# Two-layer hybrid trunk on one core: the carried part of a chunk's output enters its PSUM bank by four transposes ahead of the chunk-internal products, and its last piece is scaled earlier

## The chip, the cores and the metric

The kernel runs on 1 core of one Trainium2 chip. The metric is device time in microseconds (us) of one execution; a comparison takes the medians of several executions of both kernels on the same chip. All arithmetic is fp32, part of it as fp32r halves (see below).

## The reference, cut to what matters

One inference step of two layers over 384 rows (256 of a prompt, 8 x 16 of samples). The layer is: a modulated norm, one wide input projection, three mixers side by side (windowed attention, a Mamba-2 scan, a gated MLP over chunks), a gated merge, an output projection, then a squared-ReLU MLP. The change lies in the Mamba-2 scan:

```python
def ssd_scan(x, dt, a, bm, cm, h0):
    ...
    cb = jnp.einsum('bctgn,bcsgn->bctsg', cc, bc)
    y_intra = jnp.einsum('bctsg,bctsgk,bcsgkp->bctgkp', cb, decay, xdt)
    ...
    y_inter = jnp.einsum('bctgn,bcgkpn->bctgkp', cc, h_in) * jnp.exp(cum)[..., None]
    y = (y_intra + y_inter).reshape(bsz, s, SSM_HEADS, SSM_HEAD_DIM)
    return y, h_last.reshape(bsz, SSM_HEADS, SSM_HEAD_DIM, SSM_STATE)
```

`y_intra` is the chunk-internal part, `y_inter` the part that the carried state gives.

## The kernel before, in words

The 384 rows are three pieces of 128 columns: i = 0 and 1 are the prompt, i = 2 the eight samples. Activations lie with channels on partitions, so every projection is a row of *units*: a unit is one weight block of 128 x 1024 (`raw`, fetched by SP), split by `split` (from L142) into a high half `whi` (ACT, L147) and a low half `wlo` (DVE, L148), and used in 24 matmuls of 384 columns (in PSUM banks `acc`, three of them). Such matmuls fill TensorE nearly all the time. `mm` at L92 records almost every matmul, so the rows are told apart by their tiles.

The scan is the generator `ssd(g)`, run once for each of two head groups (g = 0, 1) in each layer. `side()` advances it by one step ahead of each unit of the branch projections (`gate`, `half_branch`) and of the z projection (the loop that ends in L1047), so that its small matmuls stand between units. In one `ssd(g)`:

- `scaled(i)` turns four x blocks by transposes (L135) and makes `xdt` (DVE, L835) and from it `xde` (POOL, L836). `bts` is the turned B; the matmuls `mx<-tm,bts` ("bts(0)", "bts(1)") take `xde[0]` and `xde[1]` to the states.
- The carried part of piece 1 is one matmul with `s0`, scaled by DVE into `yin[1]` (L858). That of piece 2 is `carried`, for n = 0 and 1, into the bank `yi`; DVE scales it into `yin[2]` (L954), before the change after the loop over the eight samples.
- `decay` builds two operands for a mask, one on POOL and one on DVE (both L878); `mask` multiplies them with `s1r` on TensorE, takes the exponential (ACT, L887) and multiplies by `cbm` (DVE, L888).
- `sample(b)` updates one sample's state: `bm` from `stack` (DVE, L919), one matmul, POOL (L922), DVE (L923), and the output by SP (L924). `stack` tiles are written by DMAs from `btr` and `xr` (L868, L869); the states `st` come by DMA (L928).
- `within(i)` makes the output of piece i in the one bank `yy`: eight products of 64 x 128 (`xdt` times mask), and for i = 1 and 2 the carried part, by four matmuls of `yin[i]` with the identity (`yy<-cn,tm`; `cn` holds the identity). DVE adds it to x (L907).

With i = 1 and 2, two groups and two layers there are eight such places, with 32 identity matmuls. After the z loop `rs = sq.rstd` makes the norm of the scan's output: matmuls `mx<-ones,sqa`, a square root on ACT (L321, L327, each with loads of function tables), matmuls `mx<-ck,ones`; then come the gates' `tanh` (L1007).

The order of all instructions on each engine's queue is set at build time by a scheduler that works through a model of the program; each queue then runs in that order. Tiles come from pools: `tm` has 11 buffers, the PSUM tags `mx` 3, `yy` 1 and `yi` 1, `stack`, `bm` and `st` two each. When a buffer is held longer, the scheduler gives later tiles other buffers, with other waits.

Of the kernel before, what the change touches and what calls it, by code (L numbers as in the profile page):

```python
# [13 lines left out]
ALU = mybir.AluOpType  # L14
# [48 lines left out]
def trunk_kernel(ctx, tc, x_in, c_in, w_ada, sm_in, gf_in, cn_in, wst, wkv, gmc, kc_in, vc_in, hs_in, cs_in,  # L63
                 y_out, kp_out, vp_out, sp_out, ks_out, vs_out, ss_out, co_out, gv_out):
    nc = tc.nc
    pe, act, dve, pool, sp = nc.tensor, nc.scalar, nc.vector, nc.gpsimd, nc.sync
# [5 lines left out]
    def nm(s):  # L72
        ids[0] += 1
        return f"{s}{ids[0]}"
# [10 lines left out]
    def yi():  # L85
        return psum("yi", 1)

    def yy():
        return psum("yy", 1)

    def mm(out, lhsT, rhs, start, stop):
        return pe.matmul(out, lhsT, rhs, start=start, stop=stop, skip_group_check=True)  # L92

    def behind(ins, other, wait=False):

        kind = mybir.DependencyClass.Sync if wait else mybir.DependencyClass.NoSync
        tc.add_manual_dep(ins.ins, other.ins.name, mybir.DependencyInfo(kind, mybir.DependencyReason.DATA), reason="behind")
# [25 lines left out]
    def const(name):  # L123
        o, w = CN[name]
        return cn[:, o:o + w]

    ident, t1, t1s, s1, s1s, sel, selq = (const(n) for n in ("ident", "t1", "t1s", "s1", "s1s", "sel", "selq"))
    cos, sin = (const(n).rearrange("p (i d) -> p i d", i=3) for n in ("cos", "sin"))

    def small(l, name):  # L130
        o, w = SM[name]
        return sm[:, l, o:o + w]
# [71 lines left out]
    def bc(ap, shape, axis):  # L204
        return ap.unsqueeze(axis).to_broadcast(list(shape))
# [270 lines left out]
    def mixers(l, pa, st, h, first):  # L476
        def tm(dt=F32):
            return pa.tile([128, 512], dt, tag="tm", name=nm("tm"), bufs=11)
# [121 lines left out]
        ecum = [ex[:, i * 16:i * 16 + 16] for i in range(3)]  # L600
# [170 lines left out]
        o = SM["conv_w"][0]  # L771
# [30 lines left out]
        def heads(ap):  # L802
            return ap.rearrange("p (h d) -> p h d", h=8)

        def hb_(ap):
            return bc(ap, (128, 8, 64), 2)

        def ssd(g):
            Bf, Cf = xs[8 + g], xs[10 + g]
            hs = slice(8 * g, 8 * g + 8)  # L810
# [8 lines left out]
            for q in range(2):  # L819
                o = cpad[:, q].rearrange("p (r q t) -> p r q t", r=4, q=2)[:, :, q]  # L820
# [7 lines left out]
            xdt, xde = [], []  # L828
# [26 lines left out]
            yin = {1: tm()}  # L855
# [7 lines left out]
            def stack(j):  # L863

                d, r = pa.tile([128, 640], F32R, tag="stack", name=nm("stack"), bufs=2), slice(32 * j, 32 * j + 32)
                df = d.bitcast(F32)
                for o, xs_, bs_ in ((0, 0, 0), (32, 1, 0), (64, 0, 1)):
                    sp.dma_start(out=df[o:o + 32, 0:512], in_=xr[xs_][r].bitcast(F32))  # L868
                    sp.dma_start(out=df[o:o + 32, 512:], in_=btr[r, bs_].bitcast(F32))  # L869
                act.copy(d[:96, 0:512], df[:96, 0:512])  # L870
                return d


            def decay(hq, i):
                h0 = 8 * g + 4 * hq
                rs = [tm(F32R).rearrange("p (h t) -> p h t", h=4) for _ in range(2)]
                for j, e in enumerate((pool, dve)):
                    e.tensor_tensor(  # L878
                        rs[j], bc(t1, (128, 4, 128), 1), bc(dtr[:, j, i, h0:h0 + 4].bitcast(F32), (128, 4, 128), 2), ALU.mult)
                return rs  # L880

            def mask(hq, i, rs):
                p = mx()
                for j in range(2):
                    mm(p, s1r, rs[j].rearrange("p h t -> p (h t)"), j == 0, j == 1)
                m = tm().rearrange("p (h t) -> p h t", h=4)
                act.activation(m, p.rearrange("p (h t) -> p h t", h=4), AF.Exp)  # L887
                return m, dve.tensor_tensor(m, m, bc(cbm[:, i], (128, 4, 128), 1), ALU.mult)  # L888

            def within(i, masks):  # L890
                p = yy()
                yb = [p[:, c * 128:(c + 1) * 128] for c in range(4)]
                ms = []
                for c in range(4):
                    for hh in range(2):
                        o = (2 * c + hh) * 64
                        ms.append(mm(yb[c][64 * hh:64 * hh + 64], xdt[i][:, o:o + 64], masks[c // 2][0][:, 2 * (c % 2) + hh], c == 0, i == 0))
                behind(ms[0], masks[1][1], True)
                for m in ms[1:]:
                    behind(m, ms[0])  # L900
                if i:
                    for c in range(4):
                        mm(yb[c], yin[i][:, c * 128:(c + 1) * 128], ident, False, True)
                for c in range(4):
                    k = 4 * g + c
                    y = xs[k][:, cols[i]]
                    dve.scalar_tensor_tensor(y, y, small(l, "dskip")[:, k:k + 1], yb[c], ALU.mult, ALU.add)  # L907


            py = yi()  # L910

            def carried(q, st):
                for j in range(4):
                    r = slice(32 * j, 32 * j + 32)
                    mm(py[r, :], cpad[:, q, r], st[:, j], q == 0, q == 1)

            def sample(b, hb, d):
                bm = pa.tile([128, 128], F32R, tag="bm", name=nm("bm"), bufs=2)
                dve.tensor_scalar(bm[:96], d[:96, 512:].bitcast(F32), selq[:96, b % 2:b % 2 + 1], None, ALU.mult)  # L919
                p = mx()  # L920
                mm(p, bm[:96], d[:96, 0:512], True, True)
                pool.tensor_tensor(heads(hb), heads(hb), hb_(decb[:, b, hs]), ALU.mult)  # L922
                dve.tensor_tensor(hb, hb, p, ALU.add)  # L923
                sp.dma_start(out=ss_out[l, :, b, half], in_=hb)  # L924
# [8 lines left out]
            masks = []  # L933
            for n in range(8):
                if n < 2:
                    carried(n, sts[n])
                if n < 4:
                    masks.append(mask(n % 2, n // 2, rs))
                    if n < 3:
                        rs = decay((n + 1) % 2, (n + 1) // 2)  # L940
                if n:
                    b = n - 1
                    sample(b, sts[b % 2][:, b // 2], ds[0])
                    if b % 2:
                        ds.pop(0)
                        if b // 2 < 2:
                            ds.append(stack(b // 2 + 2))
                if n in (2, 4):
                    within(n // 2 - 1, masks[:2])
                    masks = masks[2:]  # L950
                yield
            sample(7, sts[1][:, 3], ds[0])
            yin[2] = tm()
            dve.tensor_tensor(heads(yin[2]), heads(py), hb_(ecum[2][:, hs]), ALU.mult)  # L954
            masks = [mask(hq, 2, decay(hq, 2)) for hq in range(2)]
            yield
            within(2, masks)

        def chores():
            yield  # L960
            sums()
            turn_k()
            mix(0)
            yield
            turn_q(0)
            mix(1)
            yield
            a = (0, 0, 4, 128)
            es = scores(*a)
            turn_q(1)  # L970
            mix(2)
            yield
            turned = [turn_p(0, 4, es, kh) for kh in range(2)]
            turn_q(2)
            yield
            attended(0, 0, 4, turned)
            for g0 in (0, 2):
                es = scores(1, g0, 2, 256)
                yield
                yield  # L980
                turned = [turn_p(1, 2, es, kh) for kh in range(2)]
                yield
                attended(1, g0, 2, turned)
            yield from attn_sample()
            yield from ssd(0)
            yield from ssd(1)
# [266 lines left out]
```

## Time and profile before

| | before |
|---|---|
| median of 3 runs | 1470.42 us (1467.47 to 1470.52) |
| profiled execution | 1469.02 us, span 1467.2 us |
| mean granted TensorE clock | 0.992 |
| TensorE (PE) busy | 1437.6 us, 98% |
| VectorE (DVE), ScalarE (ACT), GpSimd (POOL) busy | 904.6, 636.0, 374.3 us |

Busy time of PE is modelled from pipelined matmuls, so 98% leaves about 30 us in which it stood idle. The rows below come from the same profiled execution. In a timeline row the first two numbers are the start and the length in us, and a bracket at the end is idle time of that engine just before, with what ended it. An fp32 matmul leaves two records, so x8 is four of them.

### The profile page before, as it was taken

What the parts mean: (1) busy time and instruction counts of PE and PEld (TensorE: products, weight loads), DVE (VectorE), ACT (ScalarE), POOL (GpSimd) and SP (SyncE); (2) the same over time, 40 slices, a digit from 0 to 9 for tenths busy, and PEclk for the clock granted to TensorE, in tenths of its full rate; (3) what the DMA queues carried; (4) which work ended last, traced back from release to release, by engine and by line L of the source; (5) the groups of instructions that cost most, each with busy time, mean ns of one, the idle gap of its engine ahead of it and who ended that gap; (6) DMA issues with size and microseconds to landing.
All of it is one profiled execution on the core that took longest, in us unless ns stands there. A gap on an engine that the chain in (4) does not pass through costs nothing. (4 is left out here: it accounts for less than half of the span.)

```text
span 1467.2 us, 22805 instructions
## 1 busy us (share of the span) xinstructions
PE 1437.6 (98%) x8656; PEld 1333.6 (91%) x8656; DVE 904.6 (62%) x1571; ACT 636.0 (43%) x1134; POOL 374.3 (26%) x553
## 2 busy tenths in 40 slices
PE   8999999999999999999999999999999999999997
PEld 6888989789999888899999888898999999999997
DVE  6688866576466855443447889575764777553332
ACT  4576633235244633323335666433343446443221
POOL 3273251440124500001116622425201352000000
PEclk9999999999999999999999999999999999999998
DMA  9573346454444678753344532355433334333331
GB/s 371 196 240 118 132 129 220 151 179 151 159 155 142 225 292 300 278 214 130 128 146 144 176 109 91 118 173 173 150 115 115 130 103 142 121 124 130 129 116 44
DMA packets 79134, 237.03 MB, mean 162 GB/s; under 512 B 9648, under 2 KB 16176, under 8 KB 79024
## 3 DMA queue, kind: packets, MB, share of 16 engines
q1 hardware_dynamic: 79024, 235.57, 47.2%
q8 instruction: 68, 1.11, 0.3%
q14 instruction: 42, 0.34, 0.1%
HBM read 219.21 MB, written 12.39 MB: 158 GB/s over the span
## 5 line engine op out<-in xcount | busy, mean ns | idle before, releaser
L148 DVE TENSOR_TENSOR wlo<-raw,whi 128x1024 fp32r<-128x1024 f32 (+1 forms) x296 | 373.9, 1265 | 227.4 <-ACT whi L147 223.8
L147 ACT CAST whi<-raw 128x1024 fp32r<-128x1024 f32 (+1 forms) x296 | 305.8, 1037 | 444.1 <-PE acc L92 415.6
L92 PE MATMUL acc<-hhi,whi 128*128 128x384 f32 x1264 | 430.6, 341 | 4.8 <-ACT tm L787 2.1
L92 PE MATMUL acc<-hhi,wlo 128*128 128x384 f32 x1264 | 429.5, 340 | 1.2 <-DVE wlo L148 1.2
L92 PE MATMUL acc<-hlo,whi 128*128 128x384 f32 x1264 | 425.9, 339 | 0.0
L92 PEld LDWEIGHTS acc<-hhi,whi 128*128 128x128 f32 x1264 | 237.8, 188 | 16.6 <-issue 4.3
L92 PEld LDWEIGHTS acc<-hhi,wlo 128*128 128x128 f32 x1264 | 237.5, 188 | 14.6 <-issue 12.4
L92 PEld LDWEIGHTS acc<-hlo,whi 128*128 128x128 f32 x1264 | 237.7, 188 | 3.6 <-issue 2.3
L92 PE MATMUL acc<-fhi,wlo 128*128 128x384 f32 x512 | 172.7, 337 | 0.0
L92 PE MATMUL acc<-fhi,whi 128*128 128x384 f32 x512 | 172.3, 337 | 0.0
L92 PE MATMUL acc<-flo,whi 128*128 128x384 f32 x512 | 172.3, 337 | 0.0
L92 PE MATMUL acc<-quad,whi 128*128 128x384 f32 (+1 forms) x576 | 153.7, 346 | 0.0
L92 PEld LDWEIGHTS acc<-quad,whi 128*128 128x128 f32 x576 | 105.9, 191 | 4.1 <-issue 2.7
L92 PE MATMUL acc<-quad,wlo 128*128 128x384 f32 (+1 forms) x288 | 98.5, 342 | 0.0
L92 PEld LDWEIGHTS acc<-fhi,wlo 128*128 128x128 f32 x512 | 96.5, 189 | 1.7 <-issue 1.7
L92 PEld LDWEIGHTS acc<-fhi,whi 128*128 128x128 f32 x512 | 96.6, 189 | 0.0
L92 PEld LDWEIGHTS acc<-flo,whi 128*128 128x128 f32 x512 | 96.6, 189 | 0.0
L385 POOL TENSOR_TENSOR rs<-x,gains 128x128 f32<-128x128 f32 x24 | 27.1, 1128 | 228.0 <-DVE x L437 227.9
L302 POOL TENSOR_TENSOR ck<-x 128x128 f32<-128x128 f32 x5 | 4.9, 982 | 257.4 <-DVE x L437 249.8
L214 ACT CAST fhi<-ck 128x384 fp32r<-128x384 f32 x64 | 32.6, 512 | 71.0 <-DVE ck L1086 71.0
L92 PEld LDWEIGHTS acc<-quad,wlo 128*128 128x128 f32 x288 | 55.2, 192 | 0.2 <-issue 0.2
L215 DVE TENSOR_TENSOR flo<-ck,fhi 128x384 fp32r<-128x384 f32 x64 | 35.7, 562 | 27.1 <-ACT fhi L214 27.0
(333 smaller groups left out, 2042.0 us busy)
## 6 DMA issues: line engine op xcount, KB each, us to landing
raw<-in_wst_dram SPq DMA_DIRECT2D x288, 512.0 KB, 3.4
early<-in_w_ada_dram SPq DMA_DIRECT2D x72, 512.0 KB, 6.2
raw<-in_w_ada_dram SPq DMA_DIRECT2D x24, 512.0 KB, 4.8
st<-in_hs_dram SPq DMA_DIRECT2D x8, 1024.0 KB, 8.5
out_ss_dram<-st SPq DMA_DIRECT2D x32, 256.0 KB, 2.2
stack<-tm SPq DMA_DIRECT2D x48, 64.0 KB, 2.0
tm<-in_gmc_dram SPq DMA_DIRECT2D x10, 256.0 KB, 3.9
raw<-in_wkv_dram SPq DMA_DIRECT2D x8, 272.0 KB, 2.7
```

What stands on the lines that cost most here:

```text
L92: return pe.matmul(out, lhsT, rhs, start=start, stop=stop, skip_group_check=True)
L147: act.copy(hi[:, :n], raw[:, :n])
L148: dve.tensor_tensor(lo[:, :n], raw[:, :n], hi[:, :n].bitcast(F32), ALU.subtract)
L214: act.copy(hi, t)
L215: dve.tensor_tensor(lo, t, hi.bitcast(F32), ALU.subtract)
L302: pool.tensor_tensor(t[:, NP:], ap[:, NP:], ap[:, NP:], ALU.mult)
L385: pool.tensor_tensor(smp(s[:, 0:128]), smp(x[:, k, NP:]), bt(a[:, 1:9]), ALU.mult)
```

## The change

`within` starts the bank with the carried part and not with the products. For i = 1 and 2 four PE transposes of `yin[i]` (a matmul with `is_transpose`) write the four quarters of the bank, and the eight products accumulate on them; the four matmuls with the identity go. For i = 0 only the products stand there, as before. For this, `yin[2]` must be there before its products, and its scaling (one DVE operation on `yi`) moves from behind the sample loop to n = 1 in it. Lines behind it are numbered one higher in the changed kernel.

```diff
@@ within(i, masks)
                 ms = []
+                if i:
+                    for c in range(4):
+                        pe.matmul(yb[c], yin[i][:, c * 128:(c + 1) * 128], ident, start=c == 0, stop=False, is_transpose=True, skip_group_check=True)
                 for c in range(4):
                     for hh in range(2):
                         o = (2 * c + hh) * 64
-                        ms.append(mm(yb[c][64 * hh:64 * hh + 64], xdt[i][:, o:o + 64], masks[c // 2][0][:, 2 * (c % 2) + hh], c == 0, i == 0))
+                        ms.append(mm(yb[c][64 * hh:64 * hh + 64], xdt[i][:, o:o + 64], masks[c // 2][0][:, 2 * (c % 2) + hh], i == 0 and c == 0, True))
                 behind(ms[0], masks[1][1], True)
                 for m in ms[1:]:
                     behind(m, ms[0])
-                if i:
-                    for c in range(4):
-                        mm(yb[c], yin[i][:, c * 128:(c + 1) * 128], ident, False, True)
@@ ssd(g), loop over n
                 if n < 2:
                     carried(n, sts[n])
+                if n == 1:
+                    yin[2] = tm()
+                    dve.tensor_tensor(heads(yin[2]), heads(py), hb_(ecum[2][:, hs]), ALU.mult)
...
             sample(7, sts[1][:, 3], ds[0])
-            yin[2] = tm()
-            dve.tensor_tensor(heads(yin[2]), heads(py), hb_(ecum[2][:, hs]), ALU.mult)
```

The scheduler puts other instructions in other places too. POOL's order stays as it was; some 90 rows of DVE, 30 of SP and 30 of ACT move, all in the two stretches of the scan. Three places follow, with the order on one engine before and now.

**TensorE, layer 0, where group 0 ends** (its last `within`, and the transposes of `scaled` of group 1; `acc` rows are unit matmuls). Before:

```order
L135 MATMUL mx_2940<-cn,xs_1774 128x128
L135 MATMUL mx_2982<-cn,xs_1569 128x128
L92 MATMUL yy_2905<-tm_2859,tm_2286 64x128 x4
L92 MATMUL yy_2905<-tm_2869,tm_2286 64x128 x4
L92 MATMUL yy_2905<-cn,tm_2850 128x128 x4
L135 MATMUL mx_2982<-cn,xs_1635 128x128
L135 MATMUL mx_2982<-cn,xs_1727 128x128
L135 MATMUL mx_2982<-cn,xs_1774 128x128
L92 MATMUL acc_3006<-quad_1087,whi_3002 128x384
```

Now, first the transposes of `yin[2]`, then, 31 rows behind, the products:

```order
L92 MATMUL acc_2872<-hhi_152,wlo_2876 128x384
L896 MATMUL yy_2905<-cn,tm_2466 128x128 x4
L92 MATMUL acc_2949<-hhi_138,whi_2952 128x384
L92 MATMUL acc_2949<-hlo_139,whi_2952 128x384
L92 MATMUL acc_2949<-hhi_138,wlo_2953 128x384
```

```order
L135 MATMUL mx_2940<-cn,xs_1774 128x128
L92 MATMUL acc_2949<-hhi_152,whi_2952 128x384
L92 MATMUL yy_2905<-tm_2859,tm_2286 64x128 x4
L92 MATMUL yy_2905<-tm_2869,tm_2286 64x128 x4
L92 MATMUL acc_2949<-hlo_153,whi_2952 128x384
L92 MATMUL acc_2949<-hhi_152,wlo_2953 128x384
L135 MATMUL mx_2982<-cn,xs_1569 128x128
```

The carried part is now turned a good unit ahead of the products, in the midst of unit matmuls, and holds the one bank `yy` from then on.

**VectorE at the same place** (`bm` from `stack`, L919; `xdt` of group 1, L835, with `tm_2945` for piece 0 and `tm_2987` for piece 1). Before:

```order
L827 TENSOR_TENSOR cbm_2933<-mx_2934,cn 128x128
L919 TENSOR_SCALAR bm_3229<-stack_3111,cn 96x128
L919 TENSOR_SCALAR bm_3279<-stack_3111,cn 96x128
L835 TENSOR_TENSOR tm_2945<-mx_2940,dt_864 128x512
L148 TENSOR_TENSOR wlo_3182<-raw_3179,whi_3181 128x1024
L907 SCALAR_TENSOR_TENSOR xs_1106<-xs_1106,sm,yy_2905 128x128
L907 SCALAR_TENSOR_TENSOR xs_1180<-xs_1180,sm,yy_2905 128x128
L907 SCALAR_TENSOR_TENSOR xs_1243<-xs_1243,sm,yy_2905 128x128
L907 SCALAR_TENSOR_TENSOR xs_1350<-xs_1350,sm,yy_2905 128x128
L835 TENSOR_TENSOR tm_2987<-mx_2982,dt_864 128x512
```

Now:

```order
L827 TENSOR_TENSOR cbm_2933<-mx_2934,cn 128x128
L835 TENSOR_TENSOR tm_2945<-mx_2940,dt_864 128x512
L919 TENSOR_SCALAR bm_3231<-stack_3111,cn 96x128
L919 TENSOR_SCALAR bm_3281<-stack_3111,cn 96x128
L907 SCALAR_TENSOR_TENSOR xs_1106<-xs_1106,sm,yy_2905 128x128
L907 SCALAR_TENSOR_TENSOR xs_1180<-xs_1180,sm,yy_2905 128x128
L907 SCALAR_TENSOR_TENSOR xs_1243<-xs_1243,sm,yy_2905 128x128
L907 SCALAR_TENSOR_TENSOR xs_1350<-xs_1350,sm,yy_2905 128x128
L835 TENSOR_TENSOR tm_2987<-mx_2982,dt_864 128x512
L148 TENSOR_TENSOR wlo_3182<-raw_3179,whi_3181 128x1024
```

The first `xdt` (L835) now stands ahead of the two `bm` and no longer behind them; the second still stands behind them, and a `wlo` that was ahead of it is now behind it.

**ScalarE, layer 1, at the norm of the scan's output** (`sd` and the `ck` of L327 are the root and its diagonal; each ACT_TABLE_LOAD is a load of a function table). Before:

```order
L147 CAST whi_11300<-raw_11298 128x1024
L301 ACTIVATE ck_11094<-xs_9142 128x256
L1045 ACTIVATE quad_10678<-xs_9142,sm 128x384
L321 ACT_TABLE_LOAD
L321 ACTIVATE sd_11104<-mx_11099,eps_72 128x3
L147 CAST whi_11338<-raw_11336 128x1024
L327 ACTIVATE ck_11107<-cn,sd_11104 128x128
L1007 ACT_TABLE_LOAD
L1007 ACTIVATE ck_11146<-acc_11115 128x384
```

Now:

```order
L301 ACTIVATE ck_11094<-xs_9142 128x256
L1046 ACTIVATE quad_10680<-xs_9142,sm 128x384
L147 CAST whi_11300<-raw_11298 128x1024
L321 ACT_TABLE_LOAD
L321 ACTIVATE sd_11104<-mx_11099,eps_72 128x3
L327 ACTIVATE ck_11107<-cn,sd_11104 128x128
L1008 ACT_TABLE_LOAD
L1008 ACTIVATE ck_11146<-acc_11115 128x384
L1008 ACTIVATE ck_11179<-acc_11148 128x384
```

A `whi` stood ahead of L301 and another between the root and its diagonal; now the first is behind the squares and the second behind the gates' L1008. On TensorE `mx<-ones,sqa` had two unit matmuls between it and `mx<-ck,ones`, and has twelve now.

## Rows read from the trace of the kernel before

**Rows 1.** Page: busy time by engine, share of the span, instructions.
```profile
PE 1437.6 (98%) x8656; PEld 1333.6 (91%) x8656; DVE 904.6 (62%) x1571; ACT 636.0 (43%) x1134; POOL 374.3 (26%) x553
```

**Rows 2.** Instructions on bank `yy` by form: duration in ns min/median/max, first and last start.
```profile
L92 PE MATMUL yy<-cn,tm x64: 274/276/378, 233.9 to 1074.8; 128*128 128x128 f32 x64
...
L135 PE MATMUL yy<-cn,s x28: 270/272/273, 518.1 to 649.3; 128*128 128x128 f32 x28
```

**Rows 3.** Timeline of PE: the first and the last of eight identity blocks, each with its successor.
```profile
233.91 1.16 PE L92 MATMUL yy<-cn,tm 128*128 128x128 f32 x8
235.00 1.06 PE L92 MATMUL acc<-raw,sc 128*32 128x256 f32 x12
...
1073.96 1.16 PE L92 MATMUL yy<-cn,tm 128*128 128x128 f32 x8
1074.88 0.42 PE L92 MATMUL acc<-hlo,whi 128*128 128x384 f32 x1
```

**Rows 4.** Timeline of PE: four fp32 transposes among unit matmuls of another stage.
```profile
518.14 0.60 PE L135 MATMUL yy<-cn,s 128*128 128x128 f32 x4
518.50 0.42 PE L92 MATMUL acc<-hhi,wlo 128*128 128x384 f32 x1
518.76 0.34 PE L92 MATMUL acc<-hhi,whi 128*128 128x384 f32 x1
518.93 0.34 PE L92 MATMUL acc<-hlo,whi 128*128 128x384 f32 x1
```

**Rows 5.** Timeline of PE, layer 0, where the second group's states begin.
```profile
268.43 1.28 PE L92 MATMUL mx<-tm,bts 128*128 128x512 f32 x2 [2.26 <-POOL tm L836]
...
273.51 1.13 PE L92 MATMUL mx<-tm,bts 128*128 128x512 f32 x2
```

**Rows 6.** Stretches: length, busy us (count) of PE, PEld, DVE, ACT, POOL; PEclk; DMA.
```profile
269.27:272.68 3.41, 3.41 (x15) 2.68 (x17) 0.94 (x3) 1.63 (x2) 2.22 (x3) 0.50 0.24 93
302.00:308.00 6.00, 5.03 (x29) 4.45 (x30) 4.49 (x9) 2.04 (x3) 2.96 (x3) 1.00 0.25 74
500.00:660.00 160.00, 159.74 (x998) 135.96 (x991) 84.40 (x137) 59.47 (x91) 2.52 (x5) 1.00 0.75 273
```

**Rows 7.** Timeline of DVE, same place.
```profile
265.27 0.48 DVE L919 TENSOR_SCALAR bm<-stack,cn 96x128 fp32r<-96x128 f32 x2 [6.85 <-DMA stack<-btr]
265.67 0.68 DVE L835 TENSOR_TENSOR tm<-mx,dt 128x512 f32<-128x512 f32 x1
...
267.40 1.11 DVE L907 SCALAR_TENSOR_TENSOR xs<-xs,sm,yy 128x128 f32<-128x128 f32 x4
```

**Rows 8.** Timeline of POOL, same place.
```profile
266.43 1.95 POOL L836 TENSOR_TENSOR tm<-tm,ex 128x512 f32<-128x512 f32 x1 [13.71 <-DVE tm L835]
269.19 1.04 POOL L836 TENSOR_TENSOR tm<-tm,ex 128x512 f32<-128x512 f32 x1 [0.81 <-DVE tm L835]
```

**Rows 9.** Timelines of DVE and PE, layer 1, the same point of the program.
```profile
1002.21 0.48 DVE L919 TENSOR_SCALAR bm<-stack,cn 96x128 fp32r<-96x128 f32 x2 [4.68 <-DMA stack<-btr]
...
1005.50 1.12 PE L92 MATMUL mx<-tm,bts 128*128 128x512 f32 x2 [0.35 <-POOL tm L836]
```

**Rows 10.** Timeline of PE at the norm of the scan's output, layer 0 and layer 1.
```profile
366.46 0.83 PE L92 MATMUL mx<-ck,ones 128*128 128x128 f32 x6
367.21 0.44 PE L92 MATMUL acc<-hhi,whi 128*128 128x384 f32 x1
...
1093.98 0.46 PE L92 MATMUL mx<-ck,ones 128*128 128x128 f32 x2 [0.52 <-DVE ck L329]
1094.72 0.71 PE L92 MATMUL mx<-ck,ones 128*128 128x128 f32 x4 [0.28 <-ACT ck L327]
1096.52 0.44 PE L92 MATMUL acc<-hhi,whi 128*128 128x384 f32 x1 [1.09 <-ACT ck L1007]
```

**Rows 11.** Timelines of POOL and PE, layer 0, group 1: a late mask.
```profile
296.31 4.61 POOL L922 TENSOR_TENSOR st<-st,ex 128x512 f32<-128x512 f32 x3
...
302.97 0.73 PE L92 MATMUL mx<-tm,s1r 128*128 128x512 f32 x2 [1.55 <-POOL tm L878]
```

## The prediction

> **What bounds the kernel now.** I read the page first: TensorE is busy 98% of the span, 1437.6 us, and no other engine over 62% [rows 1]. So the sum goes by TensorE's queue: a matmul less is worth its distance to the next start, and another engine counts only where TensorE stands idle for it. I then took the instructions on the bank `yy` by form [rows 2], for the price of the removed and the added ones; the timeline of TensorE around the eight places, for distances between starts, which are what a pipelined matmul really costs [rows 3, 4]; and the idle brackets of TensorE inside the two scan stretches, since only these can vanish or grow by a new order [rows 5, 9 to 11]. The profiled execution took 1469.02 us, 1.4 us less than the median of 1470.42; the sum is made against the first, the forecast stands on the second. A difference of 0.2%, 2.9 us, is about what can be told from no change here.
>
> **The direct part.** Removed are 32 identity matmuls in eight places, added 32 transposes. The identity matmuls leave 64 records, the 28 fp32 transposes of another stage leave 28, each 0.27 us long [rows 2]: a transpose passes once where the fp32 matmul passes twice. From start to next start an identity block takes 235.00 - 233.91 = 1.09 us at the first place and 1074.88 - 1073.96 = 0.92 at the last; the mean of the eight is 0.96 [rows 3]. Four such transposes take 518.50 - 518.14 = 0.36 us [rows 4]. The same rows show that the unit matmul behind a foreign block is followed after 0.26 us, the next after 0.17, and the order shows transposes and products now apart, with unit matmuls between: one more such break, which I put at 0.1. A place gains 0.96 - 0.36 - 0.1 = 0.5, all eight 4.0 us, all on the path. The ends: nothing, if a transpose that is accumulated on costs what the identity matmul did, and 8 x 0.6 = 4.8 without the extra break. I take 4.0, since the nearest rows are of the same operation, shape and type.
>
> One rule speaks against this. The rows first: in the stretch from 500 to 660 us, with all 28 transposes, the granted clock is 1.00, the upper level of 2.4 GHz, and TensorE is busy for 159.74 of the 160 us; the four of a block stand 0.09 us apart [rows 2, 4, 6]. The Trainium skill ("TensorE: Matmul & The Clock Gate", Part 4, on the PE-mode transpose) says that a transpose does not count as PE-busy in the way that a matmul does, so that the full clock does not engage for it, and gives about 275 ns for one in a kernel. By that figure the 32 would cost 8.8 us, an estimate, against the 7.7 that they replace, and the sum would be 5.1 worse. The trace agrees with it as the length of one (270 to 273 ns), not as its cost, and not on the clock.
>
> **`yin[2]` earlier.** The same DVE operation, 0.68 us by rows of that size [rows 7], is done once per group as before, now ahead of a `wlo` of the next units. DVE is busy 62% [rows 1] and the `wlo` are made ahead, so I cost it at nothing; without that cover, 4 x 0.68 = 2.7 us. It holds one of the 11 `tm` buffers longer, which is the second rival below.
>
> **Layer 0, where group 1 starts.** TensorE stands for 2.26 us before bts(0), for POOL's `xde[0]` [rows 5]. POOL had waited for DVE's L835, and DVE for 6.85 us on a DMA into `stack`, with two `bm` ahead of L835 on its queue [rows 7, 8]. A stretch of 3.41 us at a granted clock of 0.50 (1.2 GHz) begins 0.84 us after TensorE's restart [rows 6]; it costs at most half of itself, 1.7 us. In the new order the first L835 stands ahead of the `bm`, so `xde[0]` is there some microseconds before it is wanted: 2.26 + 1.7 = 4.0 can go. But the second L835 still stands behind the `bm`. If the DMA lands when it does now, DVE starts the `bm` at 265.27, has done them by 265.67, then four L907 (1.1) and L835 (0.68) [rows 7]: 267.4. POOL's L836 takes 1.04 to 1.95 [rows 8], so `xde[1]` is ready at 268.5 to 269.4. TensorE comes to bts(0) about a microsecond before 268.43 - 2.26 = 266.2, for what the first two places saved, and to bts(1) some 2 us later, over six unit matmuls (1.0), four transposes (0.36) and bts(0) itself (an estimate of 0.6): about 267.2. **The wait moves to bts(1) and shrinks** to between 0 (the DMA too is earlier) and 2.2 us; I take 1.3. Behind a wait of 1.55 us in layer 0 the clock stays at 1.00 [rows 6, 11], so I let the half-speed stretch go: gain 4.0 - 1.3 = 2.7 us, ends 0 and 4.0.
>
> **Layer 1, the same point.** Here the DMA ends DVE's wait before the `bm` at 1002.21 and TensorE waits only 0.35, before bts(1) [rows 9]. In the new order bts(1) comes nine unit matmuls sooner, but SP's queue also issues the DMAs from `btr` sooner, past one of the two `st` loads. If the DMA follows, the 0.35 goes; if it lands as now, `xde[1]` is ready at 1002.21 + 0.4 + 1.1 + 0.68 + 1.04 = 1005.4 at best, and TensorE, 1.6 us or more sooner there, waits about 2 us instead of 0.35. Between a gain of 0.35 and a loss of 2 I take zero.
>
> **Layer 1, the norm.** TensorE idles 0.52 + 0.28 + 1.09 = 1.89 us around `mx<-ck,ones`, because root, diagonal and the gates' `tanh` with its table load follow one another on ACT with only two unit matmuls to cover them. Layer 0 has twelve matmuls in between and no idle bracket [rows 10]. The new order gives layer 1 the twelve and takes a `whi` out of ACT's chain. I take the 1.9 us in full, with the first bracket alone, 0.5, as the lower end, should the `whi` that now precedes the table load wait for its buffer.
>
> **Not moved.** The mask wait of 1.55 us (layer 0 in [rows 11]; layer 1 has another) hangs on POOL's queue, four L922 of 5.61 us together and then L878, and POOL's order is the same: nothing.
>
> **Sum:** 4.0 + 2.7 + 0 + 1.9 = 8.6 us. From 1469.0 this gives 1460.4, from the median 1461.8: I say **1462**.
>
> **The rivals.**
> - *Only the direct part* (chance 0.22). The waits on DMA and POOL are not shortened, only met at another matmul, and the half-speed stretch falls behind one of them. For it: the whole DVE chain behind `bm` still hangs on the landing of `stack` [rows 7, 9]. Against it: in layer 0 the first L835 does leave that chain. 1470.4 - 4.0 = 1466.4.
> - *The longer-held buffer makes masks late: slower* (0.10). `yin[2]` takes a `tm` buffer over most of the sample loop; the next `decay` gets one that comes free only after a `within`, then L878, the mask matmul, exponential and L888 are late, and the products behind them stop TensorE. The price is that of such a wait now, 1.55 us [rows 11], and where the clock falls behind it 1.7 more: 3.25. Three such places eat the 8.6. There are four `ssd` runs; one in each makes 4 x 3.25 - 8.6 = +4.4: 1474.8. For it: L878 comes late on POOL already, behind 5.61 us of L922 [rows 11]. Against it: the queue of POOL is not reordered, and the products that free the buffers stand well ahead.
> - *Transposes let the clock fall: slower* (0.07). TensorE at 1.2 GHz for 3.4 us behind each of the eight places costs 8 x 1.7 = 13.6, and 13.6 - 8.6 = +5.0: 1475.4. Two or three places decide little; from seven on it is over 0.2% slower. Against it is the stretch with 28 transposes at 1.00 [rows 6]; for it, that here they come just where idle brackets are near. The rule of the Trainium skill weighed above ("TensorE: Matmul & The Clock Gate", Part 4) would bring this; the trace so far does not bear it out.
> - *The change does not do what it says* (0.06): a transpose into an accumulated bank runs in two passes like the matmul. Then only the new order counts: 1470.4 - 4.6 = 1465.8. In the trace it would show as 64 records.
>
> **How the numbers follow.** My forecast has 0.55, the rivals 0.22, 0.10, 0.07 and 0.06. The forecast's own range: all gains at their upper ends are 4.8 + 4.0 + 0.35 + 1.9 = 11.1, from the lowest run 1467.5 1456.4; at the lower ends 4.0 + 0 + 0.5 - 2, 1467.9. The range of 8 in 10 has to take in the rivals that keep only one part, with a spread of some 3 us between runs as shown: 1456 to 1470. Faster by over 0.2% (below 1467.5): 0.53 of the forecast, 0.17 of the first rival and 0.05 of the last, 0.75. Slower (above 1473.3): 0.07 of the late masks and 0.05 of the clock, 0.12. The rest, 0.13, is within 0.2%.
>
> **What would show it.** Right: `yy<-cn,tm` at L896 with 32 records, blocks of four 0.36 to 0.45 us apart from their successors; no bracket before the layer 0 bts(0), a smaller one before bts(1), no half-speed stretch at 270 us; no idle brackets around layer 1's `mx<-ck,ones`; the mask waits unchanged at 1.55. Wrong: 64 records or 0.2 us and more per transpose; brackets over 1.5 us at bts(1) in both layers; new brackets before `mx<-tm,s1r` or `yy<-tm,tm` that end on L878 or L888; or stretches at 0.50 behind L896.

## The result, and the profile after

The changed kernel takes 1460.45 us (median of 6 runs, 1455.41 to 1463.61), beside it the kernel before 1468.2 us (6 runs, 1465.8 to 1470.52): a ratio of 0.9947, 95% interval 0.9932 to 0.9962. It is 7.75 us faster. The forecast was 1462, with 1456 to 1470.

The profiled execution after is the slowest of its six: 1463.61 us, span 1461.8. The page's busy times, which answer to [rows 1]:

```profile
PE 1432.2 (98%) x8624; PEld 1329.1 (91%) x8624; DVE 908.4 (62%) x1571; ACT 635.9 (44%) x1134; POOL 380.5 (26%) x553
```

TensorE has 32 matmul records less, which is what the answer by form on bank `yy` shows (for [rows 2]; duration in ns min/median/max):

```profile
L896 PE MATMUL yy<-cn,tm x32: 270/272/327, 231.4 to 1063.0; 128*128 128x128 f32 x32
```

On TensorE's timeline (start and length in us) such a block stands in the midst of unit matmuls; this is the second of the eight, for [rows 3]:

```profile
254.89 0.60 PE L896 MATMUL yy<-cn,tm 128*128 128x128 f32 x4
255.24 0.42 PE L92 MATMUL acc<-hhi,whi 128*128 128x384 f32 x1
```

It costs 0.35 us from start to start. The idle brackets of TensorE's timeline in the two scans, for [rows 5, 9, 11], and the norm of layer 1, for [rows 10]:

```profile
270.70 1.12 PE L92 MATMUL mx<-tm,bts 128*128 128x512 f32 x2 [1.41 <-POOL tm L836]
300.61 0.73 PE L92 MATMUL mx<-tm,s1r 128*128 128x512 f32 x2 [1.58 <-POOL tm L878]
...
1003.40 1.12 PE L92 MATMUL mx<-tm,bts 128*128 128x512 f32 x2 [2.75 <-POOL tm L836]
...
1031.39 0.72 PE L92 MATMUL mx<-tm,s1r 128*128 128x512 f32 x2 [1.40 <-POOL tm L878]
...
1090.13 0.83 PE L92 MATMUL mx<-ck,ones 128*128 128x128 f32 x6
1090.88 0.45 PE L92 MATMUL acc<-hhi,whi 128*128 128x384 f32 x1
```

Layer 0's wait has moved from bts(0) to bts(1) and is smaller, the mask waits are as they were, the norm has no bracket, and layer 1's wait at bts(1) has grown from 0.35 to 2.75 us. The granted clock by stretches (length, busy us and count of PE, PEld, DVE, ACT and POOL, then the clock, the DMA share and GB/s); the first four hold all eight blocks of transposes, the last is the one stretch at half speed between start and end:

```profile
231.00:264.00 33.00, 33.00 (x226) 30.84 (x225) 18.98 (x31) 10.00 (x15) 4.52 (x4) 1.00 0.72 233
308.00:341.00 33.00, 33.00 (x220) 30.00 (x217) 25.54 (x46) 14.31 (x23) 3.59 (x3) 1.00 0.61 201
969.00:996.00 27.00, 27.00 (x181) 25.69 (x180) 16.54 (x28) 9.79 (x15) 4.53 (x4) 1.00 0.71 214
1039.00:1066.00 27.00, 27.00 (x166) 26.14 (x165) 22.72 (x39) 12.95 (x22) 3.38 (x3) 1.00 0.54 183
...
875.23:878.64 3.41, 3.41 (x13) 3.41 (x12) 3.41 (x7) 1.91 (x6) 1.97 (x3) 0.50 0.42 143
```

**Where the time went, from one trace to the other.** Layer 0's scan, from its fifth mask matmul (`mx<-tm,s1r`) to `mx<-ck,ones`, took 366.46 - 220.68 = 145.78 us and takes 363.27 - 222.34 = 140.93: 4.85 less. Layer 1's, from the last matmul that waits for L685 to the first unit behind the norm, took 1096.52 - 894.39 = 202.13 and takes 1090.88 - 892.46 = 198.42: 3.71 less. Together 8.56. Outside of them this execution lost 3.1 us: 1.66 ahead of the first scan (0.68 of it by 21 us, where the waits are longer, the rest about a second half-speed stretch, from 21.88 to 25.29 us), and 1.56 around 875 us, where half speed begins 1.3 us behind a wait that both kernels have (2.11 us, for ACT's L787).

In the two scans the waits account for 4.55 - 2.99 = 1.56 in layer 0 (2.26 + 1.55 + 0.74 before, 1.41 + 1.58 after) and for 3.79 - 4.15 = -0.36 in layer 1 (0.35 + 1.55 + 1.89 before, 2.75 + 1.40 after); each layer had a half-speed stretch of 3.41 us that is gone, up to 1.7 us each. Layer 0's is in [rows 6]; this is layer 1's, in the trace before:

```profile
1033.85:1037.26 3.41, 3.41 (x13) 3.41 (x12) 3.41 (x8) 1.43 (x2) 0.74 (x1) 0.50 0.41 125
```

What is left, 8.56 - 1.2 - 3.4 = about 4.0 us, is what these books leave for the direct part. The blocks themselves, from start to next start and without idle time, take 7.65 us in the trace before and 2.89 after, 4.76 less; about 1 us of that went back into the rows beside the places, if each half-speed stretch cost all of its 1.7.

### The profile page after: what moved, and what is told of

Same layout as the page of the kernel before. It is cut to its first block, busy times and chain, and to the rows that moved or that the text cites. A ratio compares the mean times of both kernels' runs of the same rounds, so it can differ in the third digit from the quotient of the medians.

```text
span 1461.8 us, 22741 instructions
## 1 busy us (share of the span) xinstructions
PE 1432.2 (98%) x8624; PEld 1329.1 (91%) x8624; DVE 908.4 (62%) x1571; ACT 635.9 (44%) x1134; POOL 380.5 (26%) x553
## 4 chain that ended last, share of the span: by engine, by line
PE 83%; POOL 7%; DVE 3%; issue 2%; DMA 2%; ACT 1%; SPq 0%; DVEq 0%; POOLq 0%; ACTq 0%
PE acc L92 68%; PE mx L92 7%; PE yi L92 3%; PE yy L92 3%; POOL st L922 2%; PE mx L135 1%; DMA out_ss_dram<-st 1%; DMA stack<-btr 1%; POOL hlo L357 1%; POOL ck L351 1%; DVE wlo L148 1%; POOL ck L352 1%; DVE tm L794 1%; POOL ck L349 0%; POOL tm L878 0%
```

## The experiments

All kernels below compute the whole reference. Times are medians of 4 to 12 runs each, beside 9 to 17 runs of the kernel before on the same chip (6 for the change itself). Where two versions ran beside different runs of the kernel before, their ratios to it are compared.

| version | us | before, same chip | ratio, 95% interval |
|---|---|---|---|
| the change | 1460.45 | 1468.2 | 0.9947 (0.9932 to 0.9962) |
| identity matmuls first | 1461.26 | 1467.49 | 0.9956 (0.9944 to 0.9968) |
| only `yin[2]` early | 1469.39 | 1467.49 | 1.001 (0.9998 to 1.0022) |
| `yin[2]` late | 1456.96 | 1467.49 | 0.9928 (0.9916 to 0.994) |
| change, `bm` behind `xdt` | 1455.43 | 1467.49 | 0.9921 (0.9908 to 0.9934) |
| identity first, `bm` behind `xdt` | 1461.33 | 1467.01 | 0.9963 (0.995 to 0.9977) |
| before, `bm` behind `xdt` | 1465.18 | 1467.01 | 0.9991 (0.998 to 1.0001) |
| change, `bm`, decay on DVE | 1451.43 | 1467.01 | 0.9898 (0.9881 to 0.9914) |
| change, `bm`, POOL reordered | 1452.09 | 1467.01 | 0.9899 (0.9884 to 0.9915) |
| before, `bm`, decay on DVE | 1459.98 | 1467.36 | 0.9953 (0.9939 to 0.9966) |
| `yin[2]` late, `bm` | 1456.64 | 1467.36 | 0.9928 (0.9914 to 0.9941) |
| `yin[2]` late, `bm`, decay on DVE | 1452.78 | 1467.36 | 0.9899 (0.9885 to 0.9913) |

**Identity matmuls in the place of the transposes.**

```diff
-                        pe.matmul(yb[c], yin[i][:, c * 128:(c + 1) * 128], ident, start=c == 0, stop=False, is_transpose=True, skip_group_check=True)
+                        mm(yb[c], yin[i][:, c * 128:(c + 1) * 128], ident, c == 0, False)
```

> The changed kernel with four identity matmuls in the place of the four transposes, still ahead of the products. The order on the engines stays almost that of the changed kernel (L835 of layer 0 ahead of the bm, twelve matmuls inside the norm of layer 1), so only the price of the carried part differs. My theory: a block costs 0.96 us again instead of 0.36, 8 x 0.6 = 4.8 us more than the changed kernel: 3 us faster than before. Rival (the transposes save nothing on the path, all of the gain is the new order): as fast as the changed kernel, 7 to 8 us faster than before. In its trace 64 records on yy<-cn,tm, the waits at bts(1) and in the norm as in the changed kernel.

It was 6.2 us faster than before, nearer to the rival's number than to mine, as though transposes gave nothing. Its timeline says otherwise: a block takes 254.78 - 253.97 = 0.81 us, and there is no bracket at bts(1) in either layer, where the changed kernel's profile has 4.16 us in two.

```profile
253.97 1.05 PE L92 MATMUL yy<-cn,tm 128*128 128x128 f32 x8
254.78 0.48 PE L92 MATMUL mx<-tm,s1r 128*128 128x512 f32 x1
```

Dearer blocks (6.60 us for the eight, 3.7 more) and two missing waits cancelled; my expectation had left the waits equal. Nor was the order quite the same: in layer 1 the DMAs from `btr` were issued at 988.68 us and not at 992.63, with a scan that began only 1.1 us sooner. The run alone settles neither theory.

**The first two `bm` behind the three `xdt`.** `behind` adds an order on DVE's queue and no wait.

```diff
-            xdt, xde = [], []
+            xdt, xde, scl = [], [], []
...
-                dve.tensor_tensor(heads(a), heads(p), hb_(dt[:, i, hs]), ALU.mult)
+                scl.append(dve.tensor_tensor(heads(a), heads(p), hb_(dt[:, i, hs]), ALU.mult))
...
-                dve.tensor_scalar(bm[:96], d[:96, 512:].bitcast(F32), selq[:96, b % 2:b % 2 + 1], None, ALU.mult)
+                m = dve.tensor_scalar(bm[:96], d[:96, 512:].bitcast(F32), selq[:96, b % 2:b % 2 + 1], None, ALU.mult)
+                if b < 2:
+                    behind(m, scl[2])
```

> The changed kernel with the first two bm of each scan put behind all three xdt (L835) on DVE's queue; the order on the other four engines is the same row by row. My theory: both waits at bts(1), 1.41 and 2.75 us, are DVE's queue standing behind a bm that waits for the DMA into stack; they go, and this is 4 us faster than the changed kernel, 12 us faster than before. Rival (TensorE only meets the next late thing, POOL's L836 or the masks): within 1 us of the changed kernel, with a new or longer bracket in the next 30 us.

1455.43 us: 5 us below the changed kernel's median (3.8 by the ratios) and 12 us faster than before, where 4 and 12 were expected. In the changed kernel, DVE's timeline in layer 1 shows the head of the queue:

```profile
992.68 0.69 DVE L835 TENSOR_TENSOR tm<-mx,dt 128x512 f32<-128x512 f32 x1 [2.25 <-PE mx L135]
999.21 0.48 DVE L919 TENSOR_SCALAR bm<-stack,cn 96x128 fp32r<-96x128 f32 x2 [5.83 <-DMA stack<-btr]
999.60 1.12 DVE L907 SCALAR_TENSOR_TENSOR xs<-xs,sm,yy 128x128 f32<-128x128 f32 x4
1000.64 0.68 DVE L835 TENSOR_TENSOR tm<-mx,dt 128x512 f32<-128x512 f32 x1
```

SP's timeline shows why the DMA is late. The first row is of the kernel before, the others of the changed kernel; the two rows without a line number are DMAs in its chain of waits up to bts(1), with the time from issue to landing:

```profile
992.73 2.41 SPq L869 DMA_DIRECT2D stack<-btr  x3
...
983.08 8.12 DMA out_ss_dram<-st
991.27 0.61 SPq L928 DMA_DIRECT2D st<-in_hs_dram  x1
992.63 1.95 SPq L869 DMA_DIRECT2D stack<-btr  x3
994.04 5.04 DMA stack<-btr
```

SP stands for 4.8 us, until 991.27, before the second `st` load, for a sample's state to be written out; in the kernel before it was 2.8 us. The DMAs from `btr` are queued behind that load, and the last lands at 999.1. POOL's L836, which makes `xde[1]` behind all this, took longer too (before, then after):

```profile
1004.40 1.04 POOL L836 TENSOR_TENSOR tm<-tm,ex 128x512 f32<-128x512 f32 x1 [5.75 <-DVE tm L835]
...
1001.40 1.96 POOL L836 TENSOR_TENSOR tm<-tm,ex 128x512 f32<-128x512 f32 x1 [6.90 <-DVE tm L835]
```

With the edit the last landing is about where it was, 106.1 us behind the start of layer 1's scan against 106.6; on DVE's timeline of the same place the second L835 is done where the `bm` no longer matters, and TensorE reaches bts(1) at 996.20 without a bracket:

```profile
990.64 0.69 DVE L835 TENSOR_TENSOR tm<-mx,dt 128x512 f32<-128x512 f32 x1
996.16 0.68 DVE L835 TENSOR_TENSOR tm<-mx,dt 128x512 f32<-128x512 f32 x1
996.76 0.84 DVE L919 TENSOR_SCALAR bm<-stack,cn 96x128 fp32r<-96x128 f32 x2
```

The runs also lie closer: 1455.2 to 1458.0, against 1455.4 to 1463.6 for the change alone, whose fastest run is where four of the five runs of this version are. What varies in the change may be this wait on a landing; that was not traced run by run, and the mean granted clock varies too, 0.992 in its slowest run and 0.996 in its fastest.

**Only `yin[2]` early**: the kernel before with the scaling moved to n = 1 as in the change's diff, and nothing else.

> The kernel before with only the scaling of yin[2] moved to n = 1; products first, identity matmuls last. Its order keeps the two bm ahead of L835 at layer 0's second group and two matmuls inside layer 1's norm. My theory: the early scaling by itself gives nothing: within 1.5 us of before, with the waits of 2.3 us at bts(0) and 1.9 us in the norm still there. Rival (the early scaling is what reorders the queues and brings the waits down): 3 us faster than before.

1.001 (0.9998 to 1.0022): it gives nothing, as expected. The norm's three brackets are there unchanged, and the wait at layer 0's bts(0) is 1.50 us. In layer 1 the two `bm` now stand ahead of the first L835, and TensorE waits 2.58 us before bts(0): alone, the early scaling changes an order too, to no gain.

**`yin[2]` late**: the changed kernel with the scaling put back behind the sample loop.

> The changed kernel with yin[2] scaled where it was before, behind the sample loop; transposes first. Its order has L835 ahead of the bm in layer 0 for the first piece and in layer 1 for both pieces, and twelve matmuls in layer 1's norm. My theory: starting the bank with the carried part is what moved the queues, and the early scaling cost the 2.75 us wait at layer 1's bts(1); so this is 2 to 3 us faster than the changed kernel, 10 us faster than before, and no wait at layer 1's bts(1). Rival (the transposes now wait for the late yin[2]): slower than the changed kernel, 5 us faster than before, with brackets before L896 of half a us and more.

1456.96 us, 3.5 us less than the change (2.8 by the ratios, whose intervals overlap a little), with no bracket at bts(1) and none at L896, as expected. So starting the bank with the carried part is what brought the new order in layer 0 and in the norm; the earlier scaling is not needed for it. Both waits at bts(1) came with the earlier scaling.

**Identity matmuls again, with the `bm` behind.** The two edits above together.

> The version with the two bm behind all xdt on DVE's queue, and in it identity matmuls in the place of the transposes. Neither it nor the version with transposes waits at bts(1), so the two differ by the price of the carried part alone. My theory: a block of identity matmuls ahead of the products costs 0.81 us (the run with identity matmuls first showed it), a block of transposes 0.36, 8 x 0.45 = 3.6 us: about 1459 us beside 1455.4 for the transposes. Rival (the earlier run showed it right: transposes give nothing on the path): within 1 us of 1455.4.

1461.33 us, 5.9 more than with transposes; the intervals of the ratios, 0.995 to 0.9977 and 0.9908 to 0.9934, lie apart. In the traces the two scans differ by 2.30 us (141.54 against 139.24, layer 0) and 1.88 (196.51 against 194.63, layer 1): 4.2 us for eight blocks, 3.7 of it in the blocks themselves, neither version with a half-speed stretch in a scan. The rival is out. The spans of the two traces, 1458.7 and 1453.7, lie 5.0 apart; the other 0.8 comes behind the last wait, where half speed at the program's end lasts 12.0 us against 8.8. What makes the medians differ by 5.9 is not shown beyond that.

**The kernel before with its `bm` behind.**

> The kernel before with only the first two bm put behind the three xdt on DVE's queue. My theory: the waits before bts(0) in layer 0 (2.26 us) and bts(1) in layer 1 (0.35 us) are that queue; they go, and the half-speed stretch behind the first with them: 3 to 4 us faster than before, 1464 us, with the 1.9 us in layer 1's norm left. Rival (the xdt is late by its own transposes): within 1 us of before, a bracket of 1 us and more left at bts(0).

The bracket of 2.26 at bts(0) is gone, as is the one at layer 1's bts(1), but the time fell by 1.8 us only, where 3 to 4 were expected: 0.9991 (0.998 to 1.0001), which can't be told from no change. The spans of the two traces differ by 3.9 (1467.2 and 1463.3), so the pair of traces shows more than the medians do. The two traces with the products first and the `bm` ahead (the kernel before, and `yin[2]` early) had 2.26 and 1.50 us at bts(0), one with a half-speed stretch behind it and one without: the profile that I read showed the longer of the two waits.

**Both halves of the decay on DVE**, on top of the `bm` behind.

```diff
-                for j, e in enumerate((pool, dve)):
+                for j, e in enumerate((dve, dve)):
```

> The version with the bm behind the xdt, and both halves of every decay (L878) on DVE and none on POOL. My theory: the mask waits of 1.4 us in each layer hang on POOL's L878 behind four L922; they go, 2.8 us: about 1452.6. Rival (DVE, 63% busy and with 24 more operations of about 1 us in the stretches of the scan, becomes late for the masks or the wlo): slower than 1455.4, with brackets on DVE's lines before the masks or unit matmuls.

1451.43 us, 4 us less than with the `bm` alone (3.4 by the ratios), and the lowest median here. No bracket is left in either scan; DVE rises from 909.2 to 917.2 us busy, and in the scans nothing waits for it.

**POOL reordered**, on top of the `bm` behind; in `decay` the instruction is kept as `last[j]`.

```diff
-                pool.tensor_tensor(heads(hb), heads(hb), hb_(decb[:, b, hs]), ALU.mult)
+                m = pool.tensor_tensor(heads(hb), heads(hb), hb_(decb[:, b, hs]), ALU.mult)
+                behind(m, last[0])
```

> The version with the bm behind the xdt, and each L922 of the samples put behind the decay that stands ahead of it in the program, on POOL's queue. My theory: L878 no longer stands behind four L922, so the mask waits of 1.4 us in each layer go: 2.8 us faster than 1455.4, if the samples behind it are not late. Rival (the samples' L922 now wait for a decay whose tm buffer is not free, and their L923 holds the mx banks): slower than 1455.4, with brackets before mx<-stack,bm or the masks on L922 or L923.

1452.09 us, the same gain in another way: the mask waits are gone, and a bracket of 0.42 us before the products of layer 0 is all that came. That the mask waits hang on L878 behind four L922 is shown by two different edits.

**The kernel before with both edits**, `bm` behind and decay on DVE, to see the change where neither kernel waits for DMA or POOL.

> The kernel before (products first, identity matmuls last, yin[2] late) with the two bm behind all xdt and both halves of the decay on DVE: the waits on the DMA and on POOL are out of it, as they are out of the version of the change that has both edits (1451.4 us). The difference of the two is what the change is worth without those waits. My theory: eight blocks at 0.96 instead of 0.36 (4.8, less some 0.4 to 0.8 for the extra breaks), the 1.9 us of layer 1's norm with its two matmuls inside, and 0.7 before the z unit of layer 0: 6.5 to 7 us, 1458 us. Rival (the change is worth the blocks alone, the norm's wait would go by the other edits): 1455.5 us and no bracket in the norm.

1459.98 us against 1451.43 with the change: 8.55 us, more than expected. The norm's brackets are there, so the rival is out:

```profile
1082.99 0.46 PE L92 MATMUL mx<-ck,ones 128*128 128x128 f32 x2 [0.52 <-DVE ck L329]
1083.73 0.71 PE L92 MATMUL mx<-ck,ones 128*128 128x128 f32 x4 [0.28 <-ACT ck L327]
1085.54 0.69 PE L92 MATMUL acc<-hhi,whi 128*128 128x384 f32 x1 [1.09 <-ACT ck L1009]
```

In the same trace the clock was at half speed from 1085.02 us, within the third of these waits, to 1088.43, which the expectation had not priced (a part of it; the last number but two is the granted clock):

```profile
1086.00:1088.00 2.00, 2.00 (x8) 2.00 (x8) 0.63 (x2) 0.23 (x1) 1.01 (x1) 0.50 0.63 223
```

The 0.7 at layer 0's z unit, which the expectation had in it, isn't there in this version. Not all of the difference is the change, either. The spans of the two traces, 1457.1 and 1448.5, lie 8.7 apart: 1.55 of it behind the wait for L787, where this trace has a half-speed stretch (869.98 to 873.39) and the other none, and 1.65 behind the norm, where the clock was low. That leaves 5.5, which is 1.9 of brackets and 3.6 for the blocks and the rows beside them; the expectation without its z unit was 5.9 to 6.3. So it was the clock that put the total above it.

**`yin[2]` late with the `bm` behind, and with the decay on DVE too.**

> Transposes first, yin[2] scaled late as before, and the two bm behind all xdt. Against the version with yin[2] early and the same bm (1455.4 us) it tells what the early scaling is worth where no wait at bts(1) blurs it. My theory: nothing, within 1 us of 1455.4, and of the 1457.0 without the bm edit, since that order had no wait at bts(1). Rival (the transposes wait for the late yin[2]): slower by 1 us and more than 1455.4, with brackets before L896.

> The same with both halves of the decay on DVE: the version that beats both kernels so far (1451.4 us), but with yin[2] late. My theory: the same time within 1 us, so that of the change only the transposes are needed. Rival (early scaling takes a DVE operation out of the end of the sample loop): 1 us slower and more.

1456.64 against 1455.43 and 1452.78 against 1451.43: 1.2 and 1.35 us slower, a little over the 1 us that I had set, but measured on different runs of the kernel before, and the ratios agree (0.9928 and 0.9921; 0.9899 and 0.9898). There is no bracket before L896. If the early scaling is worth anything without the wait at bts(1), it is too little to be told here.

## Why the prediction was right

By its steps, each against the pair of profiles:

- **The direct part**, 4.0 us: right. The books of the two scans leave 4.0, the scans of the two versions with the `bm` behind differ by 4.2, and the pair that waits neither for DMA nor for POOL leaves 3.6. A transpose into a bank that is accumulated on has one record and costs 0.09 us, like those of [rows 4].
- **Layer 0's second group**, 2.7: right, the wait by its mechanism and the clock by luck. The wait went to bts(1) and was 1.41 us where 1.3 was said; with the half-speed stretch gone this comes to 2.26 + 1.7 - 1.41 = 2.55. But the reason for letting the stretch go, that the clock stays up behind a wait of 1.55 us, fails in the very trace from which it was taken: in layer 1 the stretch at 0.50 from 1033.85 begins 1.8 us behind a mask wait of 1.55 us (ended at 1032.07).
- **Layer 1's second group**, taken as zero between a gain of 0.35 and a loss of 2: wrong in this profile. The step that failed is "SP's queue also issues the DMAs from `btr` sooner". SP had them further ahead in its queue, but stood 4.8 us before the `st` load where it had stood 2.8, and issued them at 992.63 (992.73 before, with a scan that began 1.9 us later). They landed 3.0 us sooner, TensorE came 4.5 us sooner, and POOL's L836 took 1.96 us and not 1.04: the wait grew by 4.5 - 3.0 + 0.9 = 2.4 to 2.75 us. My own lower case had about that size, with the landing as before and without the longer L836.
- **Layer 1's norm**, 1.9: right, all three brackets are gone. The `whi` that now precedes the table load cost nothing.
- **`yin[2]` earlier** at nothing: right as an operation, and alone it changed nothing in the time (1.001). But the prediction priced only the operation and the buffer and not the order that it gives to the queues: with the scaling late, the changed kernel has no wait at bts(1) in either layer and its median is 3.5 us lower. With the `bm` behind, early or late makes no difference that can be told.
- Not counted and found: layer 0's 0.74 us at a z unit (L1038), which went, and layer 1's half-speed stretch at 1034 us, up to 1.7, which went too.

So the scans gained 8.56 where 8.6 was said, partly since a loss of 2.4 and gains of 0.74 and 1.7 that were not in the sum cancel: the sum was better than its parts. The median moved by 7.75. The forecast of 1462 stood on 1470.42, from three runs; from the 1468.2 of six the same sum gives 1459.6.

**The rivals.** *Only the direct part*: part of it happened. In layer 0 the wait was met at another matmul, though a smaller one, and in layer 1 it grew; the rest of the gain was real. *Late masks through the longer-held buffer*: not seen, the mask waits are 1.58 and 1.40 us where they were 1.55, and the change with `yin[2]` held short has 1.55 and 1.55. *The clock falling with the transposes*: the rule of the Trainium skill that I weighed ("TensorE: Matmul & The Clock Gate", Part 4) does not show here, since in the four stretches that hold the 32 transposes the granted clock is 1.00. *Two passes*: out, 32 records.

## What to carry to other kernels

A matmul with the identity that ends an accumulation can be turned round: a transpose that starts the bank, with the products on it, costs under half (0.36 against 0.81 to 0.96 us for four), and it need not wait for the products. When an edit lets the scheduler move rows, look at every queue whose head waits on a DMA: a small operation that is wanted late (here `bm`) and stands ahead of one that is wanted soon costs its whole landing time, and an order hint without a wait took 4 to 5 us out of the changed kernel and most of its spread. Look, too, at what a moved operation does to these orders and not only at its own cost: here an earlier scaling of 0.68 us brought two waits. Price such waits from several executions where there are any, as one profile may show the worst of them, and take a kernel's waits out before comparing the price of two operations in it.

## What was not expected of the hardware

The same four identity matmuls cost 0.91 to 1.09 us behind the products of their bank and 0.81 where they stand among unit matmuls, with the same two records each.

Half-speed stretches (1.2 GHz, 3.41 us each between start and end) came behind some waits and not behind others as long or longer: behind 1.55 us in layer 1 and not behind 1.55 in layer 0 of the kernel before; behind the 2.11 us for L787 in the changed kernel's profile and not in the one before; behind the 2.26 us at layer 0's bts(0) before and not behind the 2.75 us at layer 1's bts(1) in the changed kernel. What decides it is not shown.
